# A gate block with six Strassen pairs and ten leading row blocks instead of seven and eight, and where the next block's ring begins

## The chip, the cores and the metric

The kernel runs on one core of a Trainium2 chip. The metric is the device time of one execution in microseconds (us), as a median of several runs. The engines are TensorE (PE in the profile, with PEld for its weight loads), VectorE (DVE), ScalarE (ACT), GpSimd (POOL) and SyncE (SP), which issues the loads of weights. SBUF is the on-chip memory; PSUM, with eight banks, takes the matmuls' results.

## What is computed

The reference is one layer of a bidirectional encoder for 256 positions of width 4096, all in float32. Cut to the part that matters here:

```python
h = rms_norm(x, g_mix[i])
proj = jnp.einsum('bsd,de->bse', h, w_in[i])
c_q, c_kv, k_rope, gate_a, q_b, k_b, v_b, gate_b = jnp.split(proj, split_idx, axis=-1)
...   # latent attention from c_q, c_kv, k_rope; dilated attention from q_b, k_b, v_b
y_a = rms_norm(y_a, g_out_mla[i]) * jax.nn.silu(gate_a)
y_b = rms_norm(y_b, g_out_dil[i]) * jax.nn.silu(gate_b)
x = x + jnp.einsum('bse,ed->bsd', jnp.concatenate([y_a, y_b], axis=-1), w_out[i])
gate = jax.nn.sigmoid(jnp.einsum('bsd,de->bse', rms_norm(x, g_ple[i]), w_ple_gate[i]))
x = x + ple * gate
```

The projections by `w_in`, `w_out` and `w_ple_gate` have 4096 input rows each and make up nearly all of the work. The change touches two stretches of the projection by `w_in`: the first 1024 columns of `gate_a`, and the beginning of `q_b`.

## The kernel before

**A product in three.** A float32 operand is held as two parts, hi and lo, each of a type that TensorE takes at full rate. `mm` (L130 to L135) makes one product of three matmuls: hi by hi (L133), hi by lo (L134) and lo by hi (L135). The activations are split once and kept, as stationary operands of 128x128. The weights come from memory by SP (L799, 128 rows by 1024 columns, 512 KB) into one of four raw buffers (`RAW`, L1356), and are split by `split` (L112): ACT writes hi (L115), DVE writes lo as raw minus hi (L116). Both then move through TensorE 512 columns at a time.

**Row blocks, plain and in pairs.** `Block` (L771) computes 1024 output columns for all 256 positions over 32 row blocks of the weights. A plain row block is one step with four products (banks M2, X, M3, M4), 12 matmuls. Two row blocks can instead go as a fast pair: four steps (M1; M2 and M3; M5 and M7; M6 and M4) that make seven products instead of eight in the manner of Strassen and Winograd, 21 matmuls instead of 24. A pair costs DVE more: four subtractions of 128x512 (L823) make the sums of weights T, and each of its four steps has its own split; the second step's lo is written at L838, between two of the subtractions. The sums of activations for the pairs are made beforehand by `add_sums` (L855; five additions and subtractions by the helper at L861, and one split).

**What sets the order.** `weave` (L1185) makes a string of `c` (a plain step) and `s` (a step of a pair): `lead` plain steps, then the pairs with the remaining plain steps spread between them, then `trail` plain steps:

```python
inner, out, given = 32 - 2 * n - lead - trail, "c" * lead, 0
for i in range(n):
    k = inner * (i + 1) // n - given
    given += k
    out += "c" * (k - 1) + "s" + "c" * (k > 0) + "sss"
out += "c" * trail
```

`lay` (L1201) puts the steps on the list `steps`. A second loop runs through that list: it issues the matmuls of a step, and ahead of it the loads (`fetch`, L1441) and the splits (`convert`, L1454) of the steps to come, four to five steps ahead. Every engine does its instructions in the order in which they are issued, so the order of the splits fixes ACT's and DVE's order.

**The ring.** `tiles` (L1417) takes the SBUF tiles for a step's hi and lo from the ring of its block: three tiles called wp, and for most blocks one or two extra tiles (B6 and B4 in the first query block, T5 and T6 in the gate block; some of these only after a flag is set). A running position `at[0]` moves on by one with each step and is taken modulo the length of the ring in use. A split is issued only when the step that used the tile before has been issued.

**The stages.** In order of time: 800 columns of latents in chunks; 800 more columns as a block of four pairs (`weave(range(4), 8, 4)`); the gate block of L1253 to L1256 (1024 columns, the changed one); chunks of 512 columns of the gate that alternate with the two up-projections of the latents; the six blocks of 1024 columns of L1285 to L1293 (query, key and value, twice, called q0, k0, v0, q1, k1, v1 below); the second gate in chunks; the output projection; the gate of the per-layer embedding. At a block's end DVE reads its banks: `half_way` (L885, instructions at L888, and at L891 on ACT) when the pairs are done, and `all_way` (L898, four instructions at L901) at the end; for the gate block other tasks (L627, L634) do this. The next block's first products need those banks. During the gate block DVE also computes the latents' norms in small instructions on `st` (L223 to L231, L373 to L378).

Of the kernel before, what the change touches and what calls it, by code (L numbers as in the profile page):

```python
# [78 lines left out]
def encoder_layer(ctx: ExitStack, tc: tile.TileContext, x, p, positions, g_mix, w_in, g_q_latent, w_uq,  # L79
# [62 lines left out]
    st = cp.tile([P, 128], F32, name="st")  # L142
# [12 lines left out]
    G, at = {"mix": gT[:, :32]}, 0  # L155
# [81 lines left out]
    def spawn(task):  # L237
        urgent.append(task)
# [434 lines left out]
    def d_mid(key, blk):  # L673
        def task():
            tags = D_TAGS[key]
            if len(tags) == 2:
                d = [slot(b, [NT, 512]) for b in tags]
            else:
                both = slot(tags[0], [2, NT, 512])
                d = [both[:, 0], both[:, 1]]  # L680
            D[key] = d
            if key == ("v", 1):
                E["d"] = slot("T5", [2, NT, S])
                nc.gpsimd.dma_start(E["d"], c_dist)
            half_way(blk.ps, [(rxq if key[0] == "q" else rx)[:, t:t + 1] for t in range(NT)], lambda h, t: d[h][:, t])
            flags.add(("mid", key))
            yield
        return task

    def d_done(key, blk):  # L690
        def task():
            d = D[key]
            all_way(blk.ps, [(rxq if key[0] == "q" else rx)[:, t:t + 1] for t in range(NT)], lambda h, t: d[h][:, t])
            if key == ("v", 1):
                E["t"] = slot("T4", [2, NT, S])
                for h in range(HEADS):
                    waiting.append((set(), attend(
                        h, lambda t, h=h: d_cols("q", h)[:, t], lambda t, h=h: d_cols("k", h)[:, t], None,
                        d_cols("v", h), yb_rows(h), True), 2 + h % 2))
                spawn(y_stats(1))  # L700
                spawn(split_ya())
            yield
        return task
# [54 lines left out]
    WP = ["wp"] * 3  # L758

    class Step:  # L760
# [3 lines left out]

        def __init__(self, load, split, run, needs=(), frees=0):
            self.load, self.split, self.run, self.needs, self.frees, self.after = load, split, run, needs, frees, None
            self.ring, self.flag, self.q = WP, None, Q

    Q = 512

# [84 lines left out]
    def add_sums(n, pair, dst, tmp, name, out, rest=0, first=0):  # L855

        def task():
            def two(op, d, a, b):  # L860
                nc.vector.tensor_tensor(d, a, b, op=op)  # L861

            if isinstance(tmp, tuple):
                w = [slot(b, [8, P]) for b in tmp]
            else:
                both = slot(tmp, [2, 8, P])
                w = [both[:, 0], both[:, 1]]
            for j in range(first, n):
                a, u = w[j % 2][:, :4], w[j % 2][:, 4:]
                hi, lo = (q.rearrange("p k (t c) -> p (k t) c", t=NT) for q in pair(j))  # L870
                two(ALU.add, a, plain(hi), plain(lo))
                two(ALU.add, u[:, 0], a[:, 1], a[:, 3])
                two(ALU.subtract, u[:, 1], u[:, 0], a[:, 0])
                two(ALU.subtract, u[:, 2], a[:, 1], a[:, 0])
                two(ALU.subtract, u[:, 3], a[:, 2], u[:, 1])
                yield
                d = dst(j)
                split(d[:, 0], d[:, 1], u)
                out[j] = [(d[:, 0, i], d[:, 1, i]) for i in range(4)]
                flags.add((name, j))  # L880
                for _ in range(1 + rest):
                    yield
        return task()
# [284 lines left out]
    steps = []  # L1168
# [16 lines left out]
    def weave(fast, lead, trail, e=0):  # L1185

        n = len(fast)
# [6 lines that stand above are left out]
        if e:  # L1196
            out = out[:len(out) - trail + e] + "ee" + out[len(out) - trail + e:]
        rest = [kt for kt in range(32) if kt // 2 not in fast]
        return [("fast", j) for j in fast] + [("plain", kt) for kt in rest], out

    def lay(blk, order, mid, done, ple=None, after=(), used={}):  # L1201

        pairs, shape = order
        step = {"s": iter([x for kind, j in pairs if kind == "fast" for x in blk.fast_steps(j)]),
                "c": iter([x for kind, kt in pairs if kind == "plain" for x in blk.plain_step(kt)]), "e": iter(ple or ())}
        last = shape.rindex("s")
        for i, key in enumerate(shape):
            x = next(step[key])
            x.q = blk.q
            x.ring = WP + list(after) if after != () and i > last else blk.ring  # L1210
            if key == "s":
                x.flag = used.get(shape[:i + 1].count("s") / 4)
            if i == last:
                x.after = mid
            if i == len(shape) - 1:
                x.after = done
            steps.append(x)

    def follow(tags):

        m2, x, m3, m4, m1, m5, m6, m7 = tags
        return m1, m6, m7, m5, m2, x, m4, m3

    def hook(at, f):
        assert at not in hooks
        hooks[at] = f
# [6 lines left out]
    x0_s, z0 = {}, {}  # L1233
# [9 lines left out]
    def x_pair(j):  # L1243
        return [q[:, 2 * (j % 4):2 * (j % 4) + 2] for q in xT[j // 4]]

    hook(17, lambda: spawn(add_sums(7, x_pair, z0_dst, ("T4", "B7b"), "x0_sums", x0_s, 1)))
    gated_rings = {("T4", "T7"): ("used", 5), "B4": ("gated", 2), "Al1": ("y_sums", FAST_O - 1), ("T5", "T6"): "kpe"}
    order = weave(range(4), 8, 4)
    blk = Block(w_in[:, 800:1600], lhs_x, x0_s, "x0_sums", order, lambda kt: (), EVEN, ("T2", "T3"),
                WP + [("T6", "T5")], 400)  # L1250
    lay(blk, order, late_mid(blk), late_done(blk), after=[("T2", "T3")])
    hook(len(steps), only("o", "s"))
    order = weave(range(7), 8, 2)  # L1253
    blk = Block(w_in[:, OFF_GA:OFF_GA + 1024], lhs_x, x0_s, "x0_sums", order, lambda kt: (), follow(EVEN), ("T2", "T3"),
                WP + [("T5", "T6")])
    lay(blk, order, gates_mid(blk), gates_done(blk))  # L1256
# [28 lines left out]
    for n, key in enumerate((key, i) for i in range(2) for key in "qkv"):  # L1285
        off = {"q": OFF_Q, "k": OFF_K, "v": OFF_V}[key[0]] + 1024 * key[1]
        order = weave((range(5), range(8), range(8), range(8), (4, 5, 0, 1, 2, 3, 6, 7), (0, 1, 2, 3, 6, 7))[n],
                      16 if n == 0 else 2, 2)
        ring = (["B6", "B4"], ["B4", "B6", "B0"], ["B4", "B6", "B0"], ["B4", "B6"], ["B4", ("T4", "T7")], [("T4", "T7")])[n]
        after = ((), (), ["B4", "B6"], ["B4"], [("T4", "T7")], ())[n]  # L1290
        blk = Block(w_in[:, off:off + 1024], lhs_x, x_s, "x_sums", order, lambda kt: (), tags, "B1", WP + ring)
        lay(blk, order, d_mid(key, blk), d_done(key, blk), after=after, used={2: ("used", 5)} if n == 4 else {})
        tags = follow(tags)  # L1293
    beside = [len(steps), len(steps) + 64]
    for c in range(4):
        if c == 3:
            hook(len(steps) + 8, lambda: spawn(y_sums()))
        ch = from_x(OFF_GB + 512 * c, 512, done_gate(1, c))
# [4 lines left out]
    for k in range(WIDE_O):  # L1303
# [3 lines left out]
        order = weave(*((range(4), 12, 4), (range(7), 6, 4), (range(6), 8, 4))[k])  # L1307
# [50 lines left out]
    class Old(Step):  # L1358


        def __init__(self, i, ch, j):
            self.i, self.ch, self.j, self.ring = i, ch, j, WP
            self.needs, self.after, self.flag = ch.needs(j), None, None
            kept_before = ch.keep and not ch.keep[1]
            self.load = None if kept_before else self.fetch
            self.frees = 0 if kept_before else 1
            self.own = kept_before or ch.keep and j < len(kept)
# [47 lines left out]
    at, users = [0], {}  # L1415

    def tiles(i, st):  # L1417


        ring = st.ring  # L1420
        n = at[0] % len(ring)
        if ring[n] in gated_rings and gated_rings[ring[n]] not in flags:
            n = 0
        tag = ring[n]
        seen = users.setdefault(tag, [])
        if len(seen) >= (RING if tag == "wp" else 1) and seen[-RING if tag == "wp" else -1] > ran[0]:
            return None
        at[0] = (n + 1) % len(ring)
        seen.append(i)
        shape = [st.ch.per, st.ch.n] if isinstance(st, Old) else [2, st.q]  # L1430
        if tag == "wp":
            return tuple(wp.tile([P, *shape], F32R, tag=q, name=f"{q}{i}", bufs=RING) for q in ("hi", "lo"))
        if isinstance(tag, tuple):
            return tuple(slot(q, shape, F32R) for q in tag)
        both = slot(tag, [2, *shape], F32R)
        return both[:, 0], both[:, 1]
# [57 lines left out]
    for i, step in enumerate(steps):  # L1494
# [25 lines left out]
        n = 0  # L1520
# [35 lines left out]
```

## Time and profile before

| | us |
|---|---|
| median of 3 runs | 1931.75 |
| lowest and highest | 1930.51, 1932.32 |
| profiled execution, its own time | 1930.17 |
| its span in the profile | 1928.4 |

| engine | busy us | share of the span | instructions |
|---|---|---|---|
| TensorE, matmuls | 1908.9 | 99% | 9260 |
| TensorE, weight loads | 1623.0 | 84% | 9260 |
| VectorE | 1575.7 | 82% | 2193 |
| ScalarE | 1104.2 | 57% | 1521 |
| GpSimd | 75.5 | 4% | 122 |

A page of the profile describes one execution. Busy time is the sum of the listed durations of an engine's instructions; matmuls are pipelined, so that the next one starts before the listed end of the one before. In a timeline each line has the start and the duration in us, the engine, the line of the code (L134 is line 134), the operation, its output and inputs by the program's names, and in brackets how long the engine was idle before it and whose work released it. A few matmul records are missing from a trace.

### The profile page before, as it was taken

The page shows a single profiled execution, that of the slowest core. Times are in us where ns is not written, and L with a number is a line of the kernel's source. Part 1 is how long each engine was busy: PE and PEld are TensorE (multiplying, and loading weights), DVE is VectorE, ACT ScalarE, POOL GpSimd, SP SyncE. Part 2 cuts the span into 40 slices and gives each one's busy share as a digit, 9 for nine tenths or more (in the row PEclk, how much of TensorE's full clock was granted, in tenths as well). Part 3 has the DMA queues.
Part 4 walks back from the last instruction along what each step waited for, and adds up shares of the span by engine and source line. Part 5 has one row for each costly group of instructions (what it writes and reads, how often), then busy time and mean ns, then how long its engine had stood idle before and what let it go on. Part 6 is the DMA issues. An engine that isn't in the chain of part 4 may idle for free.

```text
span 1928.4 us, 25605 instructions
## 1 busy us (share of the span) xinstructions
PE 1908.9 (99%) x9260; PEld 1623.0 (84%) x9260; DVE 1575.7 (82%) x2193; ACT 1104.2 (57%) x1521; POOL 75.5 (4%) x122
## 2 busy tenths in 40 slices
PE   9999999999999999999999999999999999999997
PEld 8998789998877888888888888888888888888887
DVE  7877966666999999999887778888896698989866
ACT  6655565564554565555556666555565455656643
POOL 1001011220000000000000010000000000000000
PEclk9999999999999999999999999999999999999998
DMA  7666655545656676666664456665766666566675
GB/s 252 193 191 195 191 172 146 147 146 163 188 183 196 210 218 196 206 198 207 210 202 134 141 161 219 198 216 171 235 192 218 187 185 219 185 209 200 210 219 177
DMA packets 143246, 370.58 MB, mean 192 GB/s; under 512 B 12020, under 2 KB 37712, under 8 KB 143120
## 3 DMA queue, kind: packets, MB, share of 16 engines
q1 hardware_dynamic: 141488, 363.90, 61.8%
q0 software_dynamic: 1632, 5.05, 0.7%
q8 instruction: 72, 1.18, 0.2%
q14 instruction: 54, 0.44, 0.1%
HBM read 364.72 MB, written 4.19 MB: 191 GB/s over the span
## 4 chain that ended last, share of the span: by engine, by line
PE 91%; DVE 6%; DMA 1%; issue 1%; ACT 1%; SPq 0%; DVEq 0%; ACTq 0%
PE m L134 19%; PE m L135 19%; PE m L133 19%; PE t L135 4%; PE t L133 4%; PE t L134 4%; PE s L134 3%; PE o L134 3%; PE o L135 3%; PE o L133 3%; PE s L135 3%; PE s L133 3%; DVE lo L116 2%; DVE B L823 1%; PE t L461 1%
## 5 line engine op out<-in xcount | busy, mean ns | idle before, releaser
L116 DVE TENSOR_TENSOR lo<-raw,hi 128x1024 fp32r<-128x1024 f32 (+3 forms) x473 | 522.3, 1110 | 206.7 <-ACT hi L115 203.9
L115 ACT ACTIVATE hi<-raw 128x1024 fp32r<-128x1024 f32 (+3 forms) x473 | 455.7, 969 | 341.9 <-PE m L135 155.4
L133 PE MATMUL m<-hi,Ah 128*128 128x512 f32 (+2 forms) x1033 | 395.1, 382 | 0.5 <-ACT Ah L125 0.5
L134 PE MATMUL m<-lo,Ah 128*128 128x512 f32 (+2 forms) x1033 | 391.1, 379 | 1.6 <-DVE lo L116 1.4
L135 PE MATMUL m<-hi,Al 128*128 128x512 f32 (+2 forms) x1031 | 388.3, 377 | 0.0
L134 PEld LDWEIGHTS m<-lo,Ah 128*128 128x128 f32 x1033 | 194.5, 188 | 36.7 <-DVE lo L116 7.9
L135 PEld LDWEIGHTS m<-hi,Al 128*128 128x128 f32 x1031 | 193.9, 188 | 32.2 <-DVE Al L127 0.2
L133 PEld LDWEIGHTS m<-hi,Ah 128*128 128x128 f32 x1033 | 194.4, 188 | 30.3 <-ACT Ah L125 0.7
L133 PE MATMUL m<-hi,B 128*128 128x512 f32 (+2 forms) x431 | 164.6, 382 | 0.0
L134 PE MATMUL m<-lo,B 128*128 128x512 f32 (+2 forms) x431 | 160.9, 373 | 0.2 <-DVE lo L116 0.2
L135 PE MATMUL m<-hi,B 128*128 128x512 f32 (+2 forms) x431 | 160.9, 373 | 0.0
L115 ACT ACTIVATE hi<-B 128x1024 fp32r<-128x1024 f32 x87 | 91.9, 1059 | 87.0 <-DVE B L823 45.2
L116 DVE TENSOR_TENSOR lo<-B,hi 128x1024 fp32r<-128x1024 f32 x87 | 105.9, 1222 | 5.9 <-ACT hi L115 2.9
L115 ACT ACTIVATE B<-raw 128x1024 fp32r<-128x1024 f32 (+1 forms) x73 | 67.5, 933 | 49.9 <-DMA raw<-in_w_in_dram 17.7
L135 PEld LDWEIGHTS m<-hi,B 128*128 128x128 f32 x431 | 80.9, 188 | 12.0
L134 PEld LDWEIGHTS m<-lo,B 128*128 128x128 f32 x431 | 81.1, 188 | 11.7 <-DVE lo L116 0.8
L133 PEld LDWEIGHTS m<-hi,B 128*128 128x128 f32 x431 | 81.0, 188 | 10.9
L116 DVE TENSOR_TENSOR B<-raw,B 128x1024 fp32r<-128x1024 f32 (+1 forms) x73 | 77.2, 1066 | 11.9 <-ACT B L115 11.1
L823 DVE TENSOR_TENSOR B<-raw,B 128x512 f32<-128x512 f32 x126 | 86.1, 683 | 0.0
L116 DVE TENSOR_TENSOR T<-t,T 128x512 fp32r<-128x512 f32 x64 | 43.9, 687 | 41.6 <-ACT T L115 41.2
L838 DVE TENSOR_TENSOR lo<-raw,hi 128x1024 fp32r<-128x1024 f32 (+1 forms) x58 | 70.0, 1206 | 2.2 <-ACT hi L836 2.2
L133 PE MATMUL m<-B,Ah 128*128 128x512 f32 (+1 forms) x178 | 66.2, 372 | 1.8 <-DVE B L901 1.8
(810 smaller groups left out, 3925.7 us busy)
## 6 DMA issues: line engine op xcount, KB each, us to landing
raw<-in_w_in_dram SPq DMA_DIRECT2D x320, 512.0 KB, 3.9
raw<-in_w_out_dram SPq DMA_DIRECT2D x128, 512.0 KB, 4.5
raw<-in_w_ple_gate_dram SPq DMA_DIRECT2D x128, 512.0 KB, 4.4
raw<-in_w_in_dram SPq DMA_DIRECT2D x63, 400.0 KB, 3.7
raw<-in_w_uq_dram SPq DMA_DIRECT2D x32, 384.0 KB, 3.3
raw<-in_w_ukv_dram SPq DMA_DIRECT2D x16, 512.0 KB, 4.2
T<-in_x_dram SPq DMA_DIRECT2D x7, 512.0 KB, 5.8
T<-in_x_dram POOLq DMA_DIRECT2D x7, 512.0 KB, 8.2
```

Source lines behind the costliest of these rows:

```text
L115: nc.scalar.activation(hi, src, AF.Copy)
L116: nc.vector.tensor_tensor(lo, src, plain(hi), op=ALU.subtract)
L133: nc.tensor.matmul(ps, ah, bh, start=start, stop=False)
L134: nc.tensor.matmul(ps, ah, bl, start=False, stop=False)
L135: nc.tensor.matmul(ps, al, bh, start=False, stop=stop)
L461: nc.tensor.transpose(tp[:, k, t * P:(t + 1) * P], e[:, t, k * P:(k + 1) * P], ident)
L823: nc.vector.tensor_tensor(dst, a, b, op=ALU.subtract)
L838: nc.vector.tensor_tensor(lo, r[1], plain(hi), op=ALU.subtract)
```

## The change

Three edits. The gate block is laid with six pairs instead of seven, and with ten plain row blocks ahead of the first pair instead of eight; the two trailing ones stay. So it has 20 plain row blocks instead of 18 and 44 steps instead of 46. The order of its steps was

    cccccccc scsss scsss scsss scsss scsss scsss cscsss cc

and is

    cccccccccc scsss scsss cscsss scsss scsss cscsss cc

The sums of activations are made for six pairs instead of seven; the earlier block that shares them uses four. And the first step of q0 sets the ring's running position to 0, its first wp tile.

```diff
-            self.ring, self.flag, self.q = WP, None, Q
+            self.ring, self.flag, self.q, self.phase = WP, None, Q, None
...
-    hook(17, lambda: spawn(add_sums(7, x_pair, z0_dst, ("T4", "B7b"), "x0_sums", x0_s, 1)))
+    hook(17, lambda: spawn(add_sums(6, x_pair, z0_dst, ("T4", "B7b"), "x0_sums", x0_s, 1)))
...
-    order = weave(range(7), 8, 2)
+    order = weave(range(6), 10, 2)
     blk = Block(w_in[:, OFF_GA:OFF_GA + 1024], lhs_x, x0_s, "x0_sums", order, lambda kt: (), follow(EVEN), ("T2", "T3"),
                 WP + [("T5", "T6")])
...
         lay(blk, order, d_mid(key, blk), d_done(key, blk), after=after, used={2: ("used", 5)} if n == 4 else {})
+        if n == 0:
+            steps[-len(order[1])].phase = 0
...
-            self.needs, self.after, self.flag = ch.needs(j), None, None
+            self.needs, self.after, self.flag, self.phase = ch.needs(j), None, None, None
...
         ring = st.ring
+        if st.phase is not None:
+            at[0] = st.phase
         n = at[0] % len(ring)
```

## The prediction

> **What bounds the kernel now.** I read the page first, then the busy time by stretches, then PE's timeline and DVE's in the stretches where the change puts its hands, then the chain of waits there. The first part of the page:
>
> ```profile
> span 1928.4 us, 25605 instructions
> PE 1908.9 (99%) x9260; PEld 1623.0 (84%) x9260; DVE 1575.7 (82%) x2193; ACT 1104.2 (57%) x1521; POOL 75.5 (4%) x122
> PEclk9999999999999999999999999999999999999998
> ```
>
> The reader is to see that TensorE is never away for long and that its clock is granted throughout. A change can then gain in two ways only: fewer matmuls, or fewer of the small waits inside the 99%. So the stretches (us; PE, PEld, DVE, ACT, POOL busy; clock, DMA share, GB/s):
>
> ```profile
> 178.00:200.00 22.00, 21.10 (x90) 16.23 (x89) 21.50 (x40) 12.75 (x15) 0.00 (x0) 1.00 0.61 174
> 200.00:242.00 42.00, 42.00 (x184) 33.98 (x183) 40.68 (x49) 24.52 (x26) 0.00 (x0) 1.00 0.64 193
> 545.00:575.00 30.00, 29.71 (x129) 23.41 (x128) 29.59 (x34) 18.65 (x22) 0.00 (x0) 1.00 0.63 192
> 575.00:600.00 25.00, 23.14 (x101) 18.47 (x100) 21.89 (x28) 10.05 (x12) 0.00 (x0) 1.00 0.60 185
> 600.00:985.00 385.00, 385.00 (x1701) 318.89 (x1700) 354.20 (x406) 218.91 (x233) 0.57 (x1) 1.00 0.68 208
> ```
>
> PE is idle in three of them: 0.9 us in the gate block (178 to 200), 0.3 near the end of the first query block (545 to 575), 1.9 at the entry of the first key block (575 to 600). In the first and third of these rows DVE is busy for 21.50 of 22 and 29.59 of 30 us: there DVE is the bound. From 600 to 985 PE is not idle at all, so nothing is to be gained there.
>
> Busy time hides part of a wait, because a matmul's listed duration (0.39) is longer than the distance to the next one. I therefore count distances between starts. Rows of the gate block (start, duration):
>
> ```profile
> 154.37 0.39 PE L133 MATMUL m<-hi,Ah 128*128 128x512 f32 x1
> 186.07 0.39 PE L133 MATMUL m<-T,Ah 128*128 128x512 f32 x1
> 187.01 0.50 PE L134 MATMUL m<-T,Ah 128*128 128x512 f32 x1 [0.55 <-DVE T L116]
> 191.03 0.39 PE L133 MATMUL m<-hi,B 128*128 128x512 f32 x1
> 191.61 0.50 PE L134 MATMUL m<-lo,B 128*128 128x512 f32 x1 [0.18 <-DVE lo L116]
> 235.06 0.39 PE L133 MATMUL m<-hi,Ah 128*128 128x512 f32 x1
> 241.18 0.39 PE L133 MATMUL m<-hi,Ah 128*128 128x512 f32 x1
> ```
>
> 235.06 to 241.18 is an undisturbed run of 27 matmuls: 0.227 us each. 154.37 is the block's first matmul and 241.18 the first of the next chunk: 86.81 us for 7 pairs of 21 and 18 row blocks of 12, that is 363 matmuls or 82.4 us. Of the other 4.4 us some 1.7 are the 14 transposes that lie in between (L316 and L395, in four groups; my estimate from their distances). The remaining **2.7 us are waits**: 187.01 comes 0.94 after 186.07 and so 0.71 late, 191.61 comes 0.58 after 191.03 and so 0.35 late, and smaller ones follow; after each, the next matmul is some 0.11 late as well.
>
> **The change part by part.** *Gate block, PE.* A fast pair is 21 matmuls, two plain row blocks 24. One pair less adds 3 matmuls: 3 x 0.227 = **+0.68 us**. PE is the bound, so nothing hides them. The sums for pair 6 (five subtractions and additions at L861, one split) go too; they lie around 100 us, in a stretch where PE does not wait, and I give them nothing.
>
> *Gate block, DVE.* Rows of DVE (start, duration):
>
> ```profile
> 182.38 0.15 DVE L373 TENSOR_TENSOR st<-st 128x2 f32<-128x2 f32 x1
> 190.26 0.17 DVE L378 TENSOR_SCALAR st<-st 128x2 f32<-128x2 f32 x1
> 192.61 0.68 DVE L823 TENSOR_TENSOR T<-raw 128x512 f32<-128x512 f32 x1
> 196.15 1.22 DVE L838 TENSOR_TENSOR lo<-raw,hi 128x1024 fp32r<-128x1024 f32 x1
> 197.28 0.68 DVE L823 TENSOR_TENSOR T<-raw,T 128x512 f32<-128x512 f32 x1
> 200.32 0.68 DVE L823 TENSOR_TENSOR T<-raw 128x512 f32<-128x512 f32 x1
> ```
>
> From one pair's first subtraction to the next pair's, 192.61 to 200.32, DVE takes 7.71 us. In that time PE has the pair and one plain block to do, 33 matmuls or 7.49. So DVE loses 0.22 with each pair that has one plain block, and has no slack with which to pay for the small operations of the latents' norms, which lie between 182.38 and 190.33 (some 2.7 us of that stretch by their distances). A plain block costs DVE one lo, 1.13 (196.15 to 197.28), against 2.72 of PE (12 x 0.227): each plain block ahead of the pairs gives DVE 1.6 us. With ten plain blocks in the lead instead of eight, DVE does two more lo's ahead of the first pair, the norms' small operations fall on one pair instead of two, and a second plain block stands ahead of the third and of the sixth pair (before: ahead of the seventh alone). I walked the changed order of DVE through with these durations: each lo is done before PE wants it, by 2.5, 2.2, 1.3 and 0.1 us in the first steps of the first pairs and by 0.7 or more afterwards. Of 2.7 us of waits 0 to 0.3 remain: **-2.5 us**, kept between 0 (the waits only move) and -2.7 (all go). With the extra product the block stands at -1.8.
>
> *Ring of split weights.* The third edit sets the running position to 0 at the first query step. With a gate block of 44 steps instead of 46 the position is 0 there anyway: the program is instruction for instruction the same without this edit. What changes is that the first query block now begins with the first of the three wp tiles where it began with the third, because two steps went. So the extra tiles (B6, later B4) fall to other steps, and a conversion that waited for a tile can be issued earlier.
>
> *First query block.* PE's and DVE's rows:
>
> ```profile
> 551.34 0.40 PE L133 MATMUL m<-hi,Ah 128*128 128x512 f32 x1
> 551.90 0.50 PE L134 MATMUL m<-lo,Ah 128*128 128x512 f32 x1 [0.16 <-DVE lo L116]
> 533.14 1.23 DVE L838 TENSOR_TENSOR B<-raw,B 128x1024 fp32r<-128x1024 f32 x1 [1.47 <-ACT B L836]
> 548.81 0.69 DVE L823 TENSOR_TENSOR B<-raw 128x512 f32<-128x512 f32 x1
> 556.65 0.69 DVE L823 TENSOR_TENSOR B<-raw 128x512 f32<-128x512 f32 x1
> ```
>
> Here too DVE's period (7.84) is longer than PE's 7.49, and 551.90 is 0.33 late; with the matmul behind it and the same twice more at 0.34 each, the waits come to 1.3. The idle 1.47 ahead of 533.14 waits for B6, which PE left about 531.8; in the new order that step has a wp tile that is free at about 529.2. DVE does not get all of it, since the two conversions behind are bound by tiles again: I take 0.4 earlier for the pairs that follow, so **-0.4** (0 to -1.3).
>
> *Entry of the first key block.* PE's rows and the chain of waits, in order of time:
>
> ```profile
> 584.94 0.39 PE L135 MATMUL m<-B,Al 128*128 128x512 f32 x1
> 587.10 0.47 PE L133 MATMUL m<-B,Ah 128*128 128x512 f32 x1 [1.77 <-DVE B L901]
> ...
> 574.49 1.41 DVE B L888 x2
> 577.99 1.14 DVE B L116
> 579.15 4.72 DMA raw<-in_w_in_dram
> 583.97 1.07 ACT hi L115
> 585.10 1.11 issue
> 586.21 2.72 DVE B L901 x4
> 592.45 0.50 PE m L134
> ```
>
> 587.10 is 1.93 late (2.16 less 0.227). It waits for an L901 that frees a bank, and L901 waits for nothing of its own: it stands on DVE behind the lo of a plain step. That lo waits for ACT's hi, hi for a load, the load for a raw buffer, the buffer for a lo that stood behind the five L888. The same chain reaches 592.45, which I count another 0.36 late. In the changed order of DVE one lo goes ahead of the five L888, and the plain step's lo goes from before the four L901 to behind them. L888 takes about 3.4 us (574.49 to 577.99), so the load is issued near 575.5 instead of 579.15; and L901 no longer waits for it. I get L901's first bank free at about 582.7 against a need at 585.2, and the plain lo done 0.2 us before its matmul wants it. Queued behind that lo are the next pair's four operations, which come 0.9 us or more before their matmuls. **-2.45 us** with the matmuls behind both waits (0 to -2.5).
>
> By the Trainium skill ("DMA: Bandwidth & Descriptors", section "Anatomy of one DMA — SWDGE (gpsimd) path", 2.0 us plus bytes over 436 GB/s) such a 512 KB load would take 3.2 us, an estimate for another queue than this one. The row has 4.72, with two more loads in flight. By the page the new order would have 1.5 us more of slack and the sum would be the same.
>
> *Elsewhere.* One lo goes behind the five L888 at the next entry, one behind an L901 near 992, one behind L1051 at the end of the gate projections, others ahead. I cost these at 0, covered by lo's that are finished 0.7 us or more early; what it costs without the cover is the third rival. No DMA is added, and SP and POOL issue what they did.
>
> *Sum:* -2.5 + 0.68 - 0.4 - 2.45 = -4.7 us. The profiled execution took 1930.17 (1.8 beside its span), so 1925.5; it lies 1.6 below the median of the runs, 1931.75, from which I count: **1927.0 us**. If every bounded term goes to its far end the sum is 0.68 - 2.7 - 1.3 - 2.5 = -5.8, 1925.9.
>
> **The rivals.**
>
> *The entry wait stays.* The plain lo's margin of 0.2 us is thin, and the load may take longer when three are in flight. Then 2 us of wait come back at a lo instead of an L901, and the sum is -1.8 - 0.4 = -2.2, with 0.3 of the gain from the earlier load: 1929.2. Against it: L901 is free of the load in the new order whatever the load takes.
>
> *PE is the bound and DVE's relief buys nothing.* For it: PE 99%. Then only +0.68 is left: 1932.4. Against it: the releaser named at 187.01 and 191.61 is DVE. The Trainium skill says to work on the most-contended engine, and that matmul busy time does not show how near TensorE is to its limit ("Perfetto Trace Analysis", section "Identifying the Most-Contended Engine"). By that rule, with PEld at 84% against DVE's 82%, a change that adds to TensorE would lose 0.68; the same page lets the bound change by stretch, and so do the rows of 178 to 200 and 545 to 575.
>
> *Slower: a lo behind evictions.* A lo that goes behind evictions is the mechanism that cost 1.93 at 587.10, and the new order does it at other entries. Rows of the entry near 992:
>
> ```profile
> 989.29 2.35 DVE L116 TENSOR_TENSOR lo<-raw,hi 128x1024 fp32r<-128x1024 f32 x2
> 991.56 0.74 DVE L901 SCALAR_TENSOR_TENSOR B<-m,st,B 128x512 f32<-128x512 f32 x1
> 994.20 1.22 DVE L116 TENSOR_TENSOR lo<-raw,hi 128x1024 fp32r<-128x1024 f32 x1
> ```
>
> Four L901 take 2.64 (991.56 to 994.20), five L888 3.4. If the moved lo's had no slack, both entries would pay in full, 6.0 us, and 4.7 more if a load were released late once: -4.7 + 6.0 = +1.3, 1933.1, up to 1937.8. It decides where a lo now comes less than the moved time before its matmul; I find 0.7 us of slack left at both. Against it also: from 600 to 985 PE has no idle time, with 31 us of DVE idle.
>
> *Not what it says.* The third edit has no effect of its own, as told; the forecast has that in it.
>
> **How the numbers follow.** A measurement of this kernel tells 0.2%, 3.9 us, from no change. Forecast 0.62 (1925.9 to 1928.5, of which 0.57 is faster by over 0.2%); entry wait stays 0.19 (1929.2, within); PE bound 0.08 (1932.4, within); moved lo's 0.11 (0.07 slower, 0.04 within). With the distance of 1 us by which runs differ: range **1924.8 to 1930.6**, which leaves out the last two. Faster 0.58, within 0.35, slower 0.07.
>
> **What would show it.** In the profile after: the gate block's distances leave under 0.5 us of waits and PE issues 9270 matmuls where it issued 9267 (records are a few fewer); the pairs near 550 wait for under 1 us; at the key block's entry L901 stands ahead of a plain lo and no PE wait of 1 us is left. It is wrong if a wait of over 0.5 us stands at that lo, if the gate block still waits for L116, or if a new wait shows behind L888 or L901 after 600.

## The result and the profile after

| | before, us | after, us | ratio, 95% interval |
|---|---|---|---|
| median of 9 runs each | 1930.37 | 1925.84 | 0.9975 (0.9965 to 0.9985) |
| once more, on another chip (17 and 9 runs) | 1929.96 | 1925.59 | 0.9976 (0.9966 to 0.9986) |

The change takes 4.5 us off, 0.25%; the profiled spans differ by 4.4 us. The page after:

```profile
span 1924.0 us, 25596 instructions
PE 1907.5 (99%) x9263; PEld 1625.2 (84%) x9263; DVE 1570.6 (82%) x2181; ACT 1103.4 (57%) x1518; POOL 75.4 (4%) x122
PEclk9999999999999999999999999999999999999999
```

TensorE has three matmuls more than before and is busy for less time: a listed duration of 0.39 grows to as much as 0.50 when the matmul had to wait. VectorE has 12 instructions less. The stretches that the prediction quoted, after (us; PE, PEld, DVE, ACT, POOL busy; clock, DMA share, GB/s):

```profile
178.00:200.00 22.00, 22.00 (x99) 18.05 (x98) 20.52 (x40) 12.29 (x15) 0.00 (x0) 1.00 0.61 185
200.00:242.00 42.00, 42.00 (x187) 34.79 (x186) 40.09 (x47) 25.30 (x27) 0.00 (x0) 1.00 0.66 205
545.00:575.00 30.00, 29.91 (x130) 23.84 (x129) 29.56 (x35) 18.97 (x23) 0.00 (x0) 1.00 0.66 203
575.00:600.00 25.00, 25.00 (x112) 20.69 (x111) 24.64 (x31) 13.04 (x15) 0.00 (x0) 1.00 0.64 197
600.00:985.00 385.00, 385.00 (x1700) 318.65 (x1699) 354.13 (x406) 217.87 (x232) 0.57 (x1) 1.00 0.67 208
```

PE's idle 0.9 us in the gate block and 1.9 at the key block's entry are gone, and the stretch behind them is as full as it was. The gate block's first matmul, and the first behind the block:

```profile
154.32 0.39 PE L133 MATMUL m<-hi,Ah 128*128 128x512 f32 x1
...
239.15 0.39 PE L133 MATMUL m<-hi,Ah 128*128 128x512 f32 x1
```

84.83 us for 366 matmuls (83.1) and the 1.7 of transposes: nothing is left for waits. Before it was 86.81. At the key block's entry, DVE, ACT's one late hi, and PE:

```profile
573.24 2.19 DVE L888 SCALAR_TENSOR_TENSOR B<-t,st,B 128x512 f32<-128x512 f32 x3
575.34 1.40 DVE L888 SCALAR_TENSOR_TENSOR B<-m,st,B 128x512 f32<-128x512 f32 x2
579.59 1.40 DVE L901 SCALAR_TENSOR_TENSOR B<-m,st,B 128x512 f32<-128x512 f32 x2
582.23 1.22 DVE L116 TENSOR_TENSOR B<-raw,B 128x1024 fp32r<-128x1024 f32 x1
...
579.54 1.06 ACT L115 ACTIVATE B<-raw 128x1024 fp32r<-128x1024 f32 x1 [4.18 <-DMA raw<-in_w_in_dram]
...
583.46 0.39 PE L133 MATMUL m<-B,Ah 128*128 128x512 f32 x1
583.69 0.40 PE L134 MATMUL m<-B,Ah 128*128 128x512 f32 x1
```

The four L901 now stand ahead of the plain step's lo (582.23). ACT still waits 4.18 us for the load, but nobody waits for ACT: the lo ends at 583.45, and the matmul that reads it starts at 583.69, on time.

Counted for all kernels alike, as the sum over neighbouring matmuls of the distance between starts beyond 0.227 us (0.18 for 400 columns, 0.17 for 384); the columns are the stretches of the gate block's pairs, the first query block's end, the key block's entry, and 1200 to 1400, which lies in the output projection and holds some 1.6 us of transposes. Each row's waits are those of one profiled execution; the medians are over all runs, and the last column is the median of the kernel before on the same chip:

| kernel | gate, us | query | entry | 1200 to 1400 | median, us | before beside it |
|---|---|---|---|---|---|---|
| before | 2.7 | 1.3 | 2.5 | 1.7 | | |
| after | 0.1 | 0.9 | 0.0 | 1.6 | 1925.84 | 1930.37 |
| 1 gate only | 0.1 | 1.3 | 1.3 | 1.7 | 1927.22 | 1929.97 |
| 2 ring only | 2.7 | 1.0 | 0.0 | 1.7 | 1927.16 | 1929.97 |
| 3 ring at 1 | 0.1 | 1.7 | 0.0 | 1.7 | 1927.10 | 1929.97 |
| 4 lo held back | 2.8 | 1.4 | 0.7 | 1.7 | 1927.95 | 1929.97 |
| 5 lead 8, trail 4 | 1.4 | 1.0 | 0.0 | 1.7 | 1927.26 | 1929.73 |
| 6 seven pairs, lead 9 | 2.3 | 1.0 | 0.0 | 3.2 | 1927.06 | 1929.73 |
| 7 gate only, again | 0.1 | 1.3 | 1.2 | 2.5 | | |
| 8 more PE instructions | 2.8 | 1.3 | 1.1 | 2.5 | 1928.88 | 1929.73 |
| 9 after, again | 0.1 | 0.9 | 0.0 | 1.6 | 1925.59 | 1929.96 |
| 10 query lead 15 | 0.1 | 0.9 | 0.0 | 1.6 | 1925.48 | 1929.96 |
| 11 query lead 13 | 0.1 | 0.0 | 0.0 | 3.3 | 1926.54 | 1929.99 |

### The profile page after: what moved, and what is told of

Its sections match the earlier page's. It is cut to its first block, busy times and chain, and to the rows that moved or that the text cites. A ratio compares the mean times of both kernels' runs of the same rounds, so it can differ in the third digit from the quotient of the medians.

```text
span 1924.0 us, 25596 instructions
## 1 busy us (share of the span) xinstructions
PE 1907.5 (99%) x9263; PEld 1625.2 (84%) x9263; DVE 1570.6 (82%) x2181; ACT 1103.4 (57%) x1518; POOL 75.4 (4%) x122
## 4 chain that ended last, share of the span: by engine, by line
PE 94%; DVE 4%; DMA 1%; issue 1%; ACT 0%; DVEq 0%; ACTq 0%; POOLq 0%
PE m L134 20%; PE m L135 20%; PE m L133 20%; PE t L135 4%; PE t L134 4%; PE t L133 4%; PE s L134 3%; PE o L134 3%; PE o L135 3%; PE o L133 3%; PE s L135 3%; PE s L133 3%; DVE lo L116 1%; PE t L461 1%; DVE B L823 1%
## 5 line engine op out<-in xcount | busy, mean ns | idle before, releaser
L116 DVE TENSOR_TENSOR lo<-raw,hi 128x1024 fp32r<-128x1024 f32 (+3 forms) x487 | 537.9, 1109 | 206.3 <-ACT hi L115 203.0
L115 ACT ACTIVATE hi<-raw 128x1024 fp32r<-128x1024 f32 (+3 forms) x487 | 469.2, 968 | 353.7 <-PE m L135 161.3
L133 PE MATMUL m<-hi,Ah 128*128 128x512 f32 (+2 forms) x1051 | 402.4, 383 | 0.0
L134 PE MATMUL m<-lo,Ah 128*128 128x512 f32 (+2 forms) x1051 | 397.5, 378 | 1.0 <-DVE lo L116 0.9
L135 PE MATMUL m<-hi,Al 128*128 128x512 f32 (+2 forms) x1049 | 395.4, 377 | 0.0
L115 ACT ACTIVATE hi<-B 128x1024 fp32r<-128x1024 f32 x75 | 79.4, 1060 | 80.5 <-DVE B L823 51.1
L116 DVE TENSOR_TENSOR lo<-B,hi 128x1024 fp32r<-128x1024 f32 x75 | 91.4, 1221 | 4.3 <-ACT hi L115 1.9
L115 ACT ACTIVATE B<-raw 128x1024 fp32r<-128x1024 f32 (+1 forms) x66 | 60.5, 925 | 49.1 <-DMA raw<-in_w_in_dram 22.8
L115 ACT ACTIVATE B<-B 128x1024 fp32r<-128x1024 f32 (+1 forms) x60 | 57.5, 958 | 42.6 <-DVE B L823 26.8
L116 DVE TENSOR_TENSOR B<-raw,B 128x1024 fp32r<-128x1024 f32 (+1 forms) x66 | 69.4, 1058 | 15.1 <-ACT B L115 15.0
```

Of the source, the lines that this page charges most:

```text
L115: nc.scalar.activation(hi, src, AF.Copy)
L116: nc.vector.tensor_tensor(lo, src, plain(hi), op=ALU.subtract)
L133: nc.tensor.matmul(ps, ah, bh, start=start, stop=False)
L134: nc.tensor.matmul(ps, ah, bl, start=False, stop=False)
L135: nc.tensor.matmul(ps, al, bh, start=False, stop=stop)
```

## The experiments

My theory was the prediction's: the gain has two parts with separate causes, one in the gate block, one in where the next block's ring begins. The rivals were that everything from the first query block on merely came earlier, and that one of the two parts did it all.

**1. The gate block alone.** From the changed kernel:

```diff
-            steps[-len(order[1])].phase = 0
+            steps[-len(order[1])].phase = 2
```

> The changed gate block, but with the ring's position set to 2 at the first query step, where it stood before the change; from there on every conversion uses the tile it used before. My theory (the gain has two parts of separate cause): the gate block keeps under 0.3 us of waits, while the first query block's 1.3 us and the key block's entry (1.93 at an L901 and 0.36 at the lo behind it) come back in full. The time is about 2.0 us below the kernel before and 2.8 above the changed one. Rival (the entry wait went because everything upstream came earlier): the entry wait stays away and the time is within 0.5 us of the changed kernel.

Ratio 0.9986 (0.9977 to 0.9995), 2.75 us below before. The gate's waits stay away and the query block's 1.3 come back, as the theory has it; the rival, with the entry wait gone, fails. But only half of the entry's wait came back. The chain of waits there (start, duration):

```profile
577.57 3.53 DMA raw<-in_w_in_dram
581.13 0.04 ACTq L115
581.16 0.05 issue
581.21 1.07 ACT hi L115
582.30 0.04 DVE lo L116
582.34 1.10 issue
583.44 2.72 DVE B L901 x4
```

It is the chain of before, link by link, with one link shorter: the load takes 3.53 us instead of 4.72. The time, 0.75 us below what was expected, goes with it. Experiments 7 and 8 go after that.

**2. The ring alone.** The kernel before, with the position set to 0:

```diff
+        if n == 0:
+            steps[-len(order[1])].phase = 0
...
+        if st.phase is not None:
+            at[0] = st.phase
```

> The kernel before with one edit: the ring's position is set to 0 at the first query step. The gate block stays at seven pairs and eight leading row blocks. My theory: the gate block keeps its 2.7 us of waits, the first query block waits for 0.9 us instead of 1.3, the key block's entry for nothing: about 2.8 us below the kernel before. Rival (the gate block's two steps less are what matters): no gain, within 0.5 us of the kernel before.

Ratio 0.9987 (0.9978 to 0.9996), 2.81 us below before, as the theory had it. PE's waits in this kernel between 178 and 242 us are those of before (us in all, times, longest):

```profile
PE m L134 <- DVE T L116: 0.5, 1, 0.5
PE m L134 <- DVE lo L116: 0.4, 2, 0.2
```

The gate block is untouched and the entry's wait is gone. So the position is worth some 2.8 us by itself; in the changed kernel the 44 steps bring it about without the third edit (the program is the same with and without it).

**3. The position at 1.** Early load as in the changed kernel, but the lo ahead of L901 as in the kernel before (`phase = 1` in the changed kernel).

> The changed kernel with the ring's position set to 1 instead of 0 at the first query step. At the key block's entry the load of the plain step's weights is then early as in the changed kernel, but its lo stands ahead of the four L901 as in the kernel before. If the late load made the wait, it stays away: 0 to 0.5 us at the entry, and the time is within 0.5 us of the changed kernel. If the order of lo and L901 alone made it, 1 to 2 us of wait stand at L901 again and the time is 1 to 2.5 us above the changed kernel.

No wait at the entry: an early load is enough, even with the lo ahead of the L901. The forecast for the time missed. It is 2.87 us below before (0.9985, 0.9977 to 0.9994) instead of some 4.4, since the first query block waits more. Two of its matmuls:

```profile
549.09 0.50 PE L134 MATMUL m<-lo,Ah 128*128 128x512 f32 x1 [0.17 <-DVE lo L116]
550.23 0.50 PE L134 MATMUL m<-lo,Ah 128*128 128x512 f32 x1 [0.17 <-DVE lo L116]
```

1.7 us in the query column and 0.4 more ahead of it: the position decides there too, and 0 is the best of the three.

**4. The lo behind L901, the load late.** The kernel before, with one split held back (step 243 is the plain step, 239 the last of q0):

```diff
+            if i == 243 and ran[0] < 239:
+                return
             got = (st.halves() if isinstance(st, Old) else None) or tiles(i, st)
```

> The kernel before with one edit: the split of the plain step at the key block's entry is issued only after the four L901, and the load stays as late as it was. If the order of lo and L901 made the wait, 587.10 is no longer late and a wait of 0.2 to 0.5 us stands at that lo in its place: about 2.0 us below the kernel before. If the late load made it, PE waits 1 to 2 us for the lo instead, and the time is within 1 us of the kernel before.

0.9991 (0.9982 to 0.9999), 2.0 us below before. The wait moves to the lo and is small:

```profile
586.22 0.39 PE L133 MATMUL m<-hi,Ah 128*128 128x512 f32 x1
586.99 0.50 PE L134 MATMUL m<-lo,Ah 128*128 128x512 f32 x1 [0.39 <-DVE lo L116]
```

0.54 late here (0.77 less 0.227) with a load of 5.03 us. So the order is enough as well, but for 0.7 us. Each of the two, the early load and the lo behind L901, breaks the chain; it takes both being wrong to pay 2 us.

**5. Fewer pairs without the lead.** The changed kernel with

```diff
-    order = weave(range(6), 10, 2)
+    order = weave(range(6), 8, 4)
```

> Six pairs as in the changed kernel, but eight leading and four trailing row blocks. If the two leading row blocks remove the waits of the gate block, those of the first two pairs come back: 1.3 to 1.9 of the 2.7 us, and the time is 1.3 to 1.9 us above the changed kernel. If the pair that is gone removes them, the gate block waits for under 0.4 us and the time is that of the changed kernel within 0.4.

1.4 us of waits, those of the first two pairs, and 0.9988 (0.9979 to 0.9997) of before, 2.1 us worse against it than the changed kernel (1.3 to 1.9 were expected):

```profile
187.07 0.50 PE L134 MATMUL m<-T,Ah 128*128 128x512 f32 x1 [0.53 <-DVE T L116]
191.67 0.50 PE L134 MATMUL m<-lo,B 128*128 128x512 f32 x1 [0.21 <-DVE lo L116]
```

The later pairs no longer wait. Up to the third pair this order is that of before, and the third pair's second plain row block is the first difference. So the two edits of the order share the gain: the longer lead takes away 1.3 us at the first two pairs, the second plain row block ahead of the third and sixth pair the rest.

**6. Seven pairs with one more leading row block.** The changed kernel with

```diff
-    hook(17, lambda: spawn(add_sums(6, x_pair, z0_dst, ("T4", "B7b"), "x0_sums", x0_s, 1)))
+    hook(17, lambda: spawn(add_sums(7, x_pair, z0_dst, ("T4", "B7b"), "x0_sums", x0_s, 1)))
...
-    order = weave(range(6), 10, 2)
+    order = weave(range(7), 9, 2)
```

> Seven pairs, nine leading row blocks, two trailing, the ring's position set to 0 at the first query step: the changed kernel without its extra 3 matmuls and with one leading row block less. My theory (each leading row block gives VectorE 1.6 us of slack): 0.6 to 1.5 us of waits are left in the gate block, less 0.68 for the matmuls, so 0.1 below to 0.8 us above the changed kernel. Rival (the pairs themselves are too dense, wherever they start): 2 us of waits or more, 1.3 us above it.

The rival holds: 2.3 us of waits are left, and the time is 0.9985 (0.9976 to 0.9994) of before, 1.9 us worse against it than the changed kernel. DVE in the lead suggests why:

```profile
170.51 1.23 DVE L116 TENSOR_TENSOR lo<-raw,hi 128x1024 fp32r<-128x1024 f32 x1 [1.50 <-ACT hi L115]
173.48 1.23 DVE L116 TENSOR_TENSOR lo<-raw,hi 128x1024 fp32r<-128x1024 f32 x1 [1.41 <-ACT hi L115]
```

DVE waits 1.4 to 1.5 us at each leading row block for ACT's hi, which waits 1.3 us for a tile that PE frees. So DVE is already as far ahead as the tiles allow, and the 1.6 us of slack of a leading row block can't be saved up for the dense pairs. Some of it helps nearby: the waits of 0.71 and 0.35 us at the first two pairs became one of 0.29 (at 189.02), but those behind add up to 1.9 us where they were 1.4.

**7. The first experiment's kernel again.**

> A second profile of the kernel of the first experiment, in which the load at the key block's entry took 3.53 us and 1.26 us of wait were left where 2.46 were expected. If the length of that load varies from execution to execution, it can be anything from 3.5 to 5 us here and the entry's waits move with it. If it depends on the program, it is 3.5 to 3.7 us again and the waits are 1.1 to 1.4 us.

3.44 us for the load and 1.2 us at the entry, much as the first time. In two executions of this program the load is short; in the two profiled executions with the load as late as before (the kernel before and 4) it is long, 4.72 and 5.03. That speaks for the program and against chance, with two executions of each. (One run, 1928.27 us, is no comparison of times.)

**8. More instructions on TensorE.** The kernel before, with matmuls split in halves of 256 columns, well ahead of the query block:

```diff
+        made[0] += 1
+        if 600 <= made[0] < 624 and ps.shape[-1] == 512:
+            for h in (slice(0, 256), slice(256, 512)):
+                nc.tensor.matmul(ps[:, h], ah, bl[:, h], start=False, stop=False)
+        else:
+            nc.tensor.matmul(ps, ah, bl, start=False, stop=False)
```

> The kernel before, with 24 matmuls of 512 columns between 350 and 480 us (my estimate of the place) split in two halves of 256, so that TensorE's instruction stream holds 48 instructions more ahead of the key block's entry; the halves cost some 0.3 us. In the trace of the kernel before, one 16 KB transfer of the instruction queue moves at 580.2 to 581.7 us, inside the load that took 4.72 us; in the first experiment it lay before the load, which took 3.53. If that transfer lengthens the load, it now comes about 5 us earlier, ahead of the load, the load takes 3.5 to 3.7 us and the entry's waits fall from 2.46 to 1.3 us: 0.9 us below the kernel before. If the load's length has another cause, it stays at 4.5 to 5 us and the time is 0.3 us above the kernel before.

The edit does less than the expectation says. It counts 24 products, but only six of them have 512 columns; these six are split, between 386 and 390 us, and TensorE gets 12 instructions more (six matmuls and six weight loads), not 48:

```profile
span 1927.7 us, 25617 instructions
...
386.00 0.39 PE L139 MATMUL m<-lo,B 128*128 128x256 f32 x2
```

DMA queues (packets, MB, share of 16 engines) while that load is under way, first before (579.15 to 583.87), then here (579.32 to 582.65):

```profile
q1 hardware_dynamic: 301, 1.11, 77.8%
q8 instruction: 1, 0.02, 2.0%
```

```profile
q1 hardware_dynamic: 182, 0.68, 67.6%
```

The chain of waits here; the helper's lines moved, L908 is L901:

```profile
579.32 3.33 DMA raw<-in_w_in_dram
582.75 1.07 ACT hi L115
583.88 1.11 issue
584.99 2.72 DVE B L908 x4
```

The instruction transfer now moves at 577.3 to 578.3, ahead of the load; the load takes 3.33 us; the entry's wait is 1.1 us instead of 2.5. The time, 0.85 us below before, is what was expected, though its interval (0.9987 to 1.0005) does not part it from no change. The two loads behind this one start 1.1 and 2.9 us after it in both kernels, so they are not the difference. The transfer came 2.9 us earlier; six matmuls are 1.4 us (6 x 0.227), so part of the shift has another cause, which stays open. It also moves without any edit: ahead of 386 us, where the two programs are alike, single transfers lie up to 1.8 us apart (88.1 and 86.3), and in 4 this one moves at 582.4, against 580.2 in the kernel before.

**9 and 10. The changed kernel again, and a plain row block moved into the query block's first pair.** The tenth is the changed kernel with 15 leading row blocks in q0:

```diff
-                      16 if n == 0 else 2, 2)
+                      15 if n == 0 else 2, 2)
```

> The changed kernel once more, beside the run that follows it on the same chip. It keeps under 0.3 us of waits in the gate block, 0.9 in the first query block and none at the key block's entry, and is 4 to 5 us below the kernel before.

> The changed kernel with one plain row block of the first query block moved from the lead into the first pair, which had none (fifteen leading row blocks instead of sixteen). The last experiments have it that a leading row block's slack can't be saved up, because VectorE waits there for a free tile; inside the pair it can be used. By that theory the 0.9 us of waits at 549 to 566 us fall to 0 to 0.5 and the time is 0.4 to 0.9 us below the changed kernel. By the rival, that each pair with one plain row block loses 0.35 us on VectorE wherever it starts, the waits stay between 0.7 and 1.5 us and the time is that of the changed kernel within 0.4.

0.9976 (0.9966 to 0.9986) and 0.9974 (0.9964 to 0.9983): the same. The rival holds, the waits stay 0.9 us. Of the row block that was moved, DVE could again not use the slack:

```profile
531.55 1.23 DVE L116 TENSOR_TENSOR lo<-B,hi 128x1024 fp32r<-128x1024 f32 x1 [0.62 <-ACT hi L115]
534.76 1.23 DVE L116 TENSOR_TENSOR lo<-B,hi 128x1024 fp32r<-128x1024 f32 x1 [1.20 <-ACT hi L115]
```

**11. Two pairs of the query block thinned out.** As the tenth, with 13.

> The changed kernel with thirteen leading row blocks in the first query block instead of sixteen; of the three, one goes into the first pair and one each ahead of the third and the fifth pair. If density sets the waits of this block (a pair with one plain row block costs VectorE 0.35 us more than TensorE), the two doubled places pay it off: of the 0.9 us at 549 to 566 us 0 to 0.4 are left, and the time is 0.5 to 0.9 us below the changed kernel, 5.0 to 5.4 below the kernel before. If the waits come from something else in that stretch (the norms of the up-projection's end, a tile), 0.7 us or more are left and the time is that of the changed kernel within 0.4.

The waits at 549 to 566 us are gone, so density it was. The time did not follow: 0.9980 (0.9971 to 0.9989) of before, some 1 us worse against it than the changed kernel. Two waits of PE are new, at 534.49 and at 1376.44:

```profile
PE t L133 <- DVE B L588: 0.5, 1, 0.5
...
PE m L736 <- DVE T L948: 0.7, 1, 0.7
```

The first is at an instruction of the up-projection's end that the earlier pairs pushed back on DVE. The second is the entry wait's pattern again, in the output projection: evictions (L928, L948) stand behind a split, and its load takes 7.70 us beside two loads of the residual. The sixth experiment has a wait of 1.4 us at the same place. Loads of 7 us and more stand beside the residual's there in most of these kernels; why only these two wait was not tried. How much of it is the kernel's own is open too: the sixth's profiled execution is the slowest of its eleven (1928.15 us, median 1927.06), and the kernel of 1 and 7 has 1.7 us in the column 1200 to 1400 in one execution and 2.5 in the other.

## Why the prediction was right, step by step

*Gate block:* +0.68 for three matmuls less 2.5 of waits was forecast, -1.8; the rows give 84.83 against 86.81, **-2.0**. What I made of it was only half right. The extra lead was to give VectorE 1.6 us for each row block; experiment 6 speaks against saving up such slack, and 5 shows that the gain comes from the lead at the first two pairs (1.3 us) and from the doubled row blocks later (1.2). The walk through the changed order had that in it, the sentence about the 1.6 us did not.

*First query block:* 0.4 forecast, **0.4** measured (1.3 to 0.9).

*Entry of the key block:* 2.45 forecast, **2.4** measured. The mechanism is shown by 2, 3 and 4. The margin of 0.2 us that I gave the plain lo is 0.24 (583.45 to 583.69). The load was forecast earlier, and it was (573.35), but it took 6.1 us with two others in flight and an instruction transfer inside (575.0 to 576.3), against 4.72 before; the lo stood behind L901 by then and did not need it sooner.

*The third edit* has no effect of its own beside the first two; by itself, in the kernel before, it brings 2.8 us.

*Elsewhere*, forecast as nothing: some 0.3 to 0.4 us came back. One wait of it is a load's:

```profile
1780.59 1.06 ACT L115 ACTIVATE B<-raw 128x1024 fp32r<-128x1024 f32 x1 [1.91 <-DMA raw<-in_w_ple_gate_dram]
1781.69 1.23 DVE L116 TENSOR_TENSOR B<-raw,B 128x1024 fp32r<-128x1024 f32 x1 [1.13 <-ACT B L115]
...
1782.56 0.39 PE L133 MATMUL m<-B,Ah 128*128 128x512 f32 x1
1782.97 0.50 PE L134 MATMUL m<-B,Ah 128*128 128x512 f32 x1
```

It costs 0.18 us with 0.11 behind it. No eviction stands ahead of this lo; it waits for ACT, and ACT for a load that took 6.61 us. In the other execution of the same kernel (9) that load took 6.11 us and the wait is not there. The third rival's mechanism did not show: lo's went behind evictions at three entries (738.31, 988.31 and 1817.00), and no matmul there waits for more than 0.1 us. The first two rivals fail on the rows above: no wait came back at the plain lo (583.69), and VectorE's relief paid, with 2.7 us of waits in the gate block down to 0.1.

*Sum:* -2.0 - 0.4 - 2.4 + 0.4 = -4.4, against -4.7. The forecast of 1927.0 counted from a median of three runs, 1931.75; with more runs that kernel's median is 1930.37, and so the changed one came out at 1925.84, within the range. It lies just under 1925.9, which the sum gave with every term at its far end, not because more was gained than forecast but because the base was 1.4 us too high. One slip in the working: by its own items the chances are 0.57 for faster and 0.36 for within, not 0.58 and 0.35.

*Why the two parts don't add.* Alone they bring 2.75 and 2.81 us, together 4.5. The gate block alone already takes 1.2 of the entry's 2.5, since its load has no instruction transfer inside; the ring takes all 2.5. What both take counts once. The prediction booked the 2.45 wholly to the ring.

## What to carry to other kernels

An in-order engine that writes a split and empties banks is read by what stands in front: a wait for an eviction may be a wait for a load, four links back, and either an earlier load or another order breaks it. Slack ahead of a dense stretch counted here only as far as tiles were free to hold the work; thin out the stretch itself. After each such edit look at every later block entry, and at more than one execution: a load that shifts or lengthens by a microsecond can open or close a wait there (0.7 to 1.4 us in single executions of two of these kernels).

## What the runs showed of the hardware

TensorE's own instruction stream competes with the weights. The page of before counts 72 transfers on the queue "instruction" with 1.18 MB, some 16 KB each; against TensorE's 18,520 matmuls and weight loads that is one for 257 of them. The 512 KB load at the entry took 4.72 and 5.03 us with one inside it (before, and 4), and 3.53, 3.44 and 3.33 without (1, 7 and 8).

The thirteen traces together bear this out beyond the entry. Take the 512 KB loads of SP that start with no other load in flight and have one or two start behind them. 845 of them with no such transfer beside them took 3.57 us in the median and never more than 4.21. 46 with one wholly inside took 3.49 to 5.11 us, 17 of them more than 4.21. So a transfer inside can cost a load a microsecond and often costs it little; what decides between the two stays open. Loads already in flight can lengthen a load as well: ahead of the entry in the kernel before, three of four loads without a transfer that started beside another one took 4.38 to 4.59 us (issued at 567.55, 569.92 and 574.60; the fourth, at 573.46, took 3.61).

The Trainium skill says that each DMA engine takes turns, packet by packet, between the queues that have work for it ("DMA: Bandwidth & Descriptors", section "Queues, rings and completion order"). No trace here shows single DMA engines; that a load is longer with another queue's transfer inside agrees with it (4.72 against 3.53 us). By the same page's figure for another queue, named in the prediction, a 512 KB load takes 3.2 us, an estimate; with no transfer inside it took 3.33 to 3.53 here.
